# First shift and scale by feature tile with five sums at once, and the SSD Silu in three parts, in a fused four-layer network on one Trainium2 core

## The chip, the cores and the metric

The kernel runs on 1 core of one Trainium2 chip, as one launch. The metric is the device time in microseconds (us) from the start to the end of an execution; less is better. Engines are named as in the profile: PE is TensorE (matmul), PEld its weight loads, DVE VectorE, ACT ScalarE, POOL GpSimd, SP the queue that issues most DMAs.

## What is computed

Two small transformer-like blocks, one after the other, on 256 context and 256 latent tokens of width 1024. Every layer begins with adaLN: shift and scale come from `silu(c) @ ada_w + ada_b`, once for the context vector and once for the latent one. The change touches the first layer (gated linear attention, GLA) and the second (a state-space mixer, SSD):

```python
def modulate(h, shift, scale):
    return h * (1 + scale) + shift

# gla_mixer, for context and latent tokens
q, k, v, g, a = jnp.split(h @ w_in, split_at, axis=-1)      # 512, 512, 1024, 1024, 32 wide
logit = jnp.einsum('blzr,zrd->zbld', a.reshape(b, l, 2, GLA_RANK), w_a2) + b_a2[:, None, None, :]
log_a = jax.nn.log_sigmoid(logit.astype(jnp.float32)) / GLA_GATE_NORM
...                                                          # scans of 4 heads in both directions
# ssd_mixer
z, xbc, dt = jnp.split(h @ w_in, [SSD_DI, SSD_DI + SSD_CONV_DIM], axis=-1)
xbc = jax.nn.silu(dwconv(xbc, conv_w, conv_b))
xs, bm, cm = jnp.split(xbc, [SSD_DI, SSD_DI + SSD_GN], axis=-1)
...                                                          # chunked scan of 8 groups
return rms_norm(y * jax.nn.silu(z), norm_g) @ w_out, (s_f, s_b)
```

## The kernel before

All weights come from HBM in pieces of 128 rows by 1024 columns of f32 (512 KB). A large product is made from three: `load` fetches a piece into `wraw`, ACT writes its rounded part `whi` (line 419), DVE the remainder `wlo` (line 420), and `mm3` adds hi by hi, lo by hi and hi by lo into one PSUM bank (lines 441 to 443). Activations are kept the same way in pairs of big tiles. A Tile scheduler turns the written program into one in-order list for each engine; tile pools with a fixed number of buffers decide when a load may be issued.

**The start** (`layer0`, `half`, `gla`, `ada`). The generator `ada` streams each adaLN matrix in chunks: chunk c holds 1024 output features and comes in 8 pieces along the 1024 inputs, into 3 buffers `araw`. A piece costs four f32 products of a 32-column stationary tile `s` with 256 moving columns (line 541), each in its own 32 columns of the array, and in the profile each is two instructions. After the 8 pieces DVE adds the bias, transposes, and copies shifts and scales to `mf` (lines 568, 570, 574). For the first layer `_ada_tiles` orders the features so that chunk 0 holds shift and scale of feature tiles 0 to 3, and chunk 1 those of tiles 4 to 7. So `half(0)` can build the first half of the modulated input `u` after 8 pieces, and `half(1)` the rest after 16 (lines 2081, 2086). Three sums are made meanwhile by `products`: `a` and head 0's `q` and `k`, each over 8 feature tiles, 72 matrix products of 128x512. The remaining adaLN chunks are fed in steps of one piece by `fill`, which counts them in `nstep`.

**GLA.** Then come the decay logits of head 0 (`logits`, line 829), v and g of head 0 (192 products of 256 columns), and four scans. `weave(scan(h), gemm(h + 1), 0.7, 0.3)` sets 0.7 steps of the next head's projections (`gemm_ws` for q and k, 48 products of 512 columns; `gemm_xs` for v and g, 192 of 256) and 0.3 adaLN pieces behind each step of the scan, so that PE has other work while ACT, DVE and POOL make what the scan needs. What is left over is appended behind the scan.

**SSD.** The same holds for 8 groups with `weave(scan(g), gemm(g + 1), 1.1, 0.3)`. `gemm(g)` projects x and the B part (through a five-tap convolution, lines 1193 to 1198, into `FZ[g]`, columns 0 to 1535), C (1536 to 1791) and z (1792 to 2303, copied by ACT, line 1212). `scan(g)` begins with one Silu over all 2304 columns (line 1220). Then twelve PE transposes of x and B follow (line 1229) in four groups of three, each evicted by ACT (line 1230), and everything else of the scan hangs on these. The group before ends with a gating on POOL (line 1315) and a Square on ACT (line 1346, `ysq`).

## Time and profile before

| | |
|---|---|
| runs shown | 2644.35, 2653.82, 2659.15 us (median 2653.82) |
| profiled execution | 2649.63 us, span of its instructions 2647.8 us |
| mean granted PE clock | 0.981 |
| busy PE, PEld, DVE, ACT, POOL | 2509.8, 2052.2, 1939.2, 1273.6, 632.1 us |
| start, to the last of the 72 products | 0 to 62.5 us |
| logits, v and g of head 0 | 62.8 to 87.8 us |
| scan of head 0, to the first product of the next scan | 87.8 to 161.0 us |
| SSD scans | about 828 to 1160 us |

All times in the rows are from the start of the span. Busy time of PE counts an instruction up to a modelled end, and matmuls overlap, so the step from one start to the next is the better measure of what a product costs in a row. A number in brackets behind a row is the idle time of that engine just before, with what ended it.

### The profile page before, as it was taken

Reading aid. Unit: us, or ns where it says so; the run is one execution under the profiler, and the core shown is the slowest. Engines: PE = TensorE matmul, PEld = TensorE weight load, DVE = VectorE, ACT = ScalarE, POOL = GpSimd, SP = SyncE. Lnnn points to the kernel's source line nnn. Section 1 sums busy time; section 2 is a strip of 40 time slices with the busy share of each in tenths; the row PEclk is TensorE's granted clock in tenths of the full one; section 3 lists DMA queues with packets and bytes.
Section 4 is the critical chain, followed back from the end, with each engine's and each line's share of the span. In section 5 each row is a group of like instructions: output and inputs, shape, how many; then the busy total and the mean of one; then the engine's idle time right before and its main releaser. Section 6 shows DMA issues by size and latency. Waiting matters only on the chain. (4 is left out here: it accounts for less than half of the span.)

```text
span 2647.8 us, 38382 instructions
## 1 busy us (share of the span) xinstructions
PE 2509.8 (95%) x14350; PEld 2052.2 (78%) x14350; DVE 1939.2 (73%) x2999; ACT 1273.6 (48%) x2027; POOL 632.1 (24%) x517
## 2 busy tenths in 40 slices
PE   6999999999999999889999999999998998999998
PEld 3877668887778777769988778888887776888886
DVE  3566787799988777776566457756448777999987
ACT  2433444222246666745544344322235445877875
POOL 1122334032332233323224023112114331000000
PEclk8999999999999999989999999999999998999999
DMA  8344565666652222255553224656534126999995
GB/s 278 122 140 138 186 212 189 224 219 205 201 182 77 88 85 68 80 175 188 183 179 105 87 80 160 199 187 207 181 98 158 56 73 211 337 333 352 333 334 217
DMA packets 137507, 471.67 MB, mean 178 GB/s; under 512 B 16544, under 2 KB 21792, under 8 KB 137056
## 3 DMA queue, kind: packets, MB, share of 16 engines
q1 hardware_dynamic: 131264, 458.34, 51.9%
q10 hardware_dynamic: 6048, 10.80, 1.2%
q8 instruction: 115, 1.88, 0.3%
q14 instruction: 80, 0.66, 0.1%
HBM read 467.96 MB, written 1.11 MB: 177 GB/s over the span
## 5 line engine op out<-in xcount | busy, mean ns | idle before, releaser
L419 ACT ACTIVATE whi<-wraw 128x1024 fp32r<-128x1024 f32 x472 | 492.0, 1047 | 567.3 <-PE b L443 235.7
L420 DVE TENSOR_TENSOR wlo<-wraw,whi 128x1024 fp32r<-128x1024 f32 x472 | 588.6, 1256 | 221.1 <-ACT whi L419 216.7
L441 PE MATMUL b<-whi,big 128*128 128x512 f32 (+1 forms) x1696 | 599.6, 355 | 9.6 <-DVE xn L1405 4.4
L442 PE MATMUL b<-wlo,big 128*128 128x512 f32 (+1 forms) x1696 | 590.0, 348 | 6.0 <-DVE wlo L420 6.0
L443 PE MATMUL b<-whi,big 128*128 128x512 f32 (+1 forms) x1696 | 588.9, 347 | 0.6 <-POOL big L420 0.5
L441 PE MATMUL b<-big,whi 128*128 128x512 f32 (+1 forms) x1512 | 540.2, 359 | 8.7 <-ACT big L419 5.7
L443 PE MATMUL b<-big,wlo 128*128 128x512 f32 (+1 forms) x1512 | 531.0, 352 | 6.5 <-DVE wlo L420 6.5
L442 PE MATMUL b<-big,whi 128*128 128x512 f32 (+1 forms) x1512 | 532.4, 352 | 2.4 <-POOL big L420 2.2
L441 PEld LDWEIGHTS b<-whi,big 128*128 128x128 f32 x1696 | 323.6, 191 | 61.7 <-issue 14.4
L442 PEld LDWEIGHTS b<-wlo,big 128*128 128x128 f32 x1696 | 324.0, 191 | 46.7 <-DVE wlo L420 9.6
L443 PEld LDWEIGHTS b<-whi,big 128*128 128x128 f32 x1696 | 323.6, 191 | 40.3 <-issue 1.8
L441 PEld LDWEIGHTS b<-big,whi 128*128 128x128 f32 x1512 | 290.2, 192 | 56.2 <-issue 10.4
L443 PEld LDWEIGHTS b<-big,wlo 128*128 128x128 f32 x1512 | 290.8, 193 | 43.9 <-DVE wlo L420 8.2
L442 PEld LDWEIGHTS b<-big,whi 128*128 128x128 f32 x1512 | 291.1, 193 | 39.6 <-POOL big L420 5.0
L559 DVE SCALAR_TENSOR_TENSOR aacc<-wraw,s,aacc 128x1024 f32<-128x1024 f32 x161 | 233.0, 1474 | 40.3 <-DMA wraw<-in_ada 39.9
L420 DVE TENSOR_TENSOR wlo<-big,whi 128x1024 fp32r<-128x1024 f32 (+1 forms) x157 | 184.5, 1197 | 18.1 <-ACT whi L419 15.3
L420 POOL TENSOR_TENSOR big<-ut,big 128x256 fp32r<-128x256 f32 x101 | 106.3, 1061 | 381.4 <-ACT big L419 380.5
L419 ACT ACTIVATE whi<-big 128x1024 fp32r<-128x1024 f32 (+1 forms) x157 | 160.5, 1034 | 33.5 <-PE b L443 27.9
L420 POOL TENSOR_TENSOR big<-hr,big 128x512 fp32r<-128x512 f32 (+1 forms) x64 | 84.8, 1326 | 343.1 <-ACT big L419 314.4
L1198 DVE SCALAR_TENSOR_TENSOR FZ<-xp,vecs,FZ 128x512 f32<-128x512 f32 (+1 forms) x128 | 110.8, 866 | 11.3 <-ACT FZ L1196 10.1
L419 ACT ACTIVATE big<-ut 128x256 fp32r<-128x256 f32 x156 | 62.4, 413 | 85.8 <-DVE ut L676 28.1
L761 DVE TENSOR_TENSOR yt<-b,gate 128x512 f32<-128x512 f32 x92 | 63.0, 685 | 25.0 <-PE b L443 22.1
(449 smaller groups left out, 3524.4 us busy)
## 6 DMA issues: line engine op xcount, KB each, us to landing
big<-in_moe SPq DMA_DIRECT2D x148, 512.0 KB, 6.2
wraw<-in_f SPq DMA_DIRECT2D x136, 512.0 KB, 4.2
wraw<-in_ada SPq DMA_DIRECT2D x120, 512.0 KB, 4.3
araw<-in_ada SPq DMA_DIRECT2D x72, 512.0 KB, 4.4
wraw<-in_moe SPq DMA_DIRECT2D x72, 512.0 KB, 6.6
wraw<-in_g SPq DMA_DIRECT2D x68, 512.0 KB, 3.9
Hc<-in_moe SPq DMA_DIRECT2D x36, 512.0 KB, 6.4
wraw<-in_gla_o SPq DMA_DIRECT2D x16, 512.0 KB
```

The lines of the kernel that those rows point to most:

```text
L419: self.nc.scalar.activation(hi, t, AF.Copy)
L420: (eng or self.nc.gpsimd).tensor_tensor(lo, t, hi, op=OP.subtract)
L441: mm(ps, a[0], b[0], start=first, stop=False)
L442: mm(ps, a[0], b[1], start=False, stop=False)
L443: mm(ps, a[1], b[0], start=False, stop=last)
L559: nc.vector.scalar_tensor_tensor(acc[v], raw, s, acc[v], op0=OP.mult, op1=OP.add)
L761: nc.vector.tensor_mul(y, ps, gt)
L1198: V.scalar_tensor_tensor(o, xp[:, :ns, k:k + 256], w(k), o, op0=OP.mult, op1=OP.add)
```

## The change

`_ada_tiles` goes; all adaLN chunks are in plain order, and the first two, (0, 0) and (0, 1), are no longer made by `ada` (`nstep` starts at 16). A new array `head` holds the same 2048 features by feature tile: for tile k two pieces (half the inputs each) with the 128 shifts and 128 scales of that tile. `head_load` fetches them through seven buffers: the three `araw` and four that later serve the exponents (`eq`, `ek`). `head` makes 32 products of 64 moving columns for a tile (16 a piece), and DVE adds, transposes and copies 64 columns. `begin(k)` and `make` build feature tile k of `u` at once, both token halves by one ACT and one DVE instruction (before: two of each half as wide, every other tile's by POOL). Five sums are open at once: `a` and q and k of heads 0 and 1, so `products(k)` is 15 matrix products, 120 in all. Heads 0 and 1 then bring only v and g to the weave: 48 products of 512 columns leave the scan of head 0. In `ssd` the Silu of a group is three instructions: x and B, C, z.

```diff
+    def head_load(self, k, pool):
+        ts = []
+        for h in range(2):
+            n = (2 * k + h) % 7 - 3
+            ts.append(self.ar.tile([128, 1024], F32, name="araw") if n < 0 else
+                      pool.tile([128, 1024], F32, name="hraw", tag=("eq", "ek")[n % 2], bufs=2))
+            self.nc.sync.dma_start(ts[h], self.A["head"][k, h])
+        return ts
+
+    def head(self, k, ts, bias):
+        o = slice(64 * k, 64 * k + 64)
+        ps = self.adb.rearrange("p a b -> p (a b)")
+        for r in range(8):
+            for q in range(4):
+                t = ts[r // 4].rearrange("p (r q n) -> p r q n", r=4, q=4)
+                nc.tensor.matmul(ps[32 * q:32 * q + 32, o], self.s[0][:, r, :], t[:, r % 4, q, :], start=r == 0, stop=r == 7)
+        ev = self.tmp.tile([128, 256], F32, name="ut", bufs=3)[:, :64]
+        nc.vector.tensor_add(ev, ps[:, o], bias[:, o])
+        tr = self.tmp.tile([128, 256], F32, name="ut", bufs=3)[:, :64]
+        nc.vector.transpose(out=tr, in_=ev)
+        nc.vector.tensor_copy(self.mf[0][:, k:k + 9:8, :], tr.rearrange("p (a b) -> p a b", a=2)[:, :, 0:2])
...
-            if h:
+            if h > 1:
                 yield from self.gemm_ws(self.A["gla_qk"][h], u, ev)
...
-        first = gemm(0)
-        next(first)
-        b = [self.bank(self.pat), self.bank(self.pmm), self.bank(self.pmm)]
+        first = [gemm(h) for h in range(2)]
+        b = [self.bank(p) for p in (self.pat, self.pmm, self.pmm, self.pat, self.ptp)]
...
+        def products(k):
             for m, ps in enumerate(b):
+                h, j = (m - 1) // 2, (m - 1) % 2
+                self.mm3(ps, ws["a"](128 * k, 128) if m == 0 else ws[h, k // 4](256 * (k % 4) + 128 * j, 128),
+                         (u[0][:, k, :], u[1][:, k, :]), k == 0, k == 7)
+        make = {}
+        for k in range(3):
+            make[k] = begin(k)
+            weights(k)
+        for k in range(8):
+            make[k]()
+            if k:
+                products(k - 1)
+            if k < 5:
+                make[k + 3] = begin(k + 3)
+            if k in (1, 3):
+                weights(k // 2 + 3)
+        products(7)
...
-            self.weave(scan(h), gemm(h + 1), *PACE[0])
+            self.weave(scan(h), gemm(h + 1) if h else first[1], *PACE[0])
...
-            nc.scalar.activation(F, F, AF.Silu)
+            for o in (slice(0, 1536), slice(1536, 1792), slice(1792, 2304)):
+                nc.scalar.activation(F[:, o], F[:, o], AF.Silu)
...
+            def make():
+                self.head(k, ts, bias)
+                sc = self.sm.tile([128, 2], F32, name="sc0")
+                nc.vector.tensor_scalar(sc, self.mf[0][:, 8 + k, :], 1.0, None, op0=OP.add)
+                t = self.tmp.tile([128, 512], F32, name="xr", tag="y2k", bufs=3)
                 for p in range(2):
                     s = slice(256 * p, 256 * p + 256)
+                    nc.vector.tensor_scalar(t[:, s], xT[:, k, s], sc[:, p:p + 1], self.mf[0][:, k, p:p + 1], op0=OP.mult, op1=OP.add)
+                self.split(u[0][:, k, :], u[1][:, k, :], t, nc.vector)
```

In the lists below a name's number tells one buffer from another, and line numbers behind the change are higher by 2 in the helpers. The queue of SP at the start, before: the piece of `a`, the 8 pieces of chunk 0, the transposed input `xT`, head 0's first q and k weights, the 8 pieces of chunk 1.

```order
L431 DMA wraw<-in_gla_a 128x1024
L546 DMA araw<-in_ada 128x1024
L549 DMA abias<-in_adab 128x256
L546 DMA araw<-in_ada 128x1024 x7
L2079 DMA big_131<-in_xT 128x2048
L2089 DMA big_131<-in_xT 128x2048
L431 DMA wraw<-in_gla_qk 128x1024
L546 DMA araw<-in_ada 128x1024
L549 DMA abias<-in_adab 128x256
L546 DMA araw<-in_ada 128x1024 x7
L431 DMA wraw<-in_gla_qk 128x1024
```

The same place now:

```order
L592 DMA araw<-in_head 128x1024 x2
L2119 DMA big_131<-in_xT 128x1024
L433 DMA wraw<-in_gla_a 128x1024
L592 DMA araw<-in_head 128x1024
L592 DMA hraw<-in_head 128x1024
L433 DMA wraw<-in_gla_qk 128x1024
L592 DMA hraw<-in_head 128x1024 x2
L2119 DMA big_131<-in_xT 128x1024
L433 DMA wraw<-in_gla_qk 128x1024
L592 DMA hraw<-in_head 128x1024
L592 DMA araw<-in_head 128x1024 x3
L2119 DMA big_131<-in_xT 128x1024
```

The sequence now goes tile by tile, two pieces of `head` each, with `xT` in quarters and the five weight pieces in between.

PE near the end of the scan of head 0, before: the products of `out` (926), the logits of the next head (829), and projections of head 1 (441 to 443) between them.

```order
L926 MATMUL b<-big_134,AT 128x256
L926 MATMUL b<-S,QS 128x256
L829 MATMUL b<-wa_428,aT 64x128 x8
L441 MATMUL b<-whi,big_132 128x256
L442 MATMUL b<-wlo,big_132 128x256
L443 MATMUL b<-whi,big_133 128x256
L441 MATMUL b<-whi,big_132 128x256
L442 MATMUL b<-wlo,big_132 128x256
L443 MATMUL b<-whi,big_133 128x256
```

The same place now (951 is `out`, 854 the logits, 543 an adaLN piece, 909 the scores):

```order
L951 MATMUL b<-big_136,AT 128x256
L951 MATMUL b<-S,QS 128x256
L951 MATMUL b<-big_136,AT 128x256
L951 MATMUL b<-S,QS 128x256
L854 MATMUL b<-wa_700,aT 64x128 x8
L543 MATMUL ada<-araw,s_98 32x256 x4
L854 MATMUL b<-wa_700,aT 64x128 x8
L909 MATMUL b<-eq,ek 64x64 x10
L909 MATMUL b<-eq,big_136 64x64 x2
L909 MATMUL b<-big_136 64x64 x2
```

The projections of head 1 that stood here have moved ahead: the scan's own products and adaLN pieces follow each other directly.

ACT where an SSD group begins, before (1196 starts a convolution, 1278 writes the decay masks, 1212 evicts z):

```order
L1196 ACTIVATE FZ<-xp,vecs 128x256
L1278 ACTIVATE R<-tge,TH 128x128 x2
L1212 ACTIVATE FZ<-b 128x256
L419 ACTIVATE whi<-wraw 128x1024
L1346 ACTIVATE ysq<-big_6904 128x512
L419 ACTIVATE whi<-wraw 128x1024
L1212 ACTIVATE FZ<-b 128x256
L1220 ACT_TABLE_LOAD
L1220 ACTIVATE FZ<-FZ 128x2304
L1230 ACTIVATE big_6956<-b 128x384 x3
```

The same place now (1233, 1316, 1249, 1268 and 1384 are the former 1196, 1278, 1212, 1230 and 1346):

```order
L1233 ACTIVATE FZ<-xp,vecs 128x256
L1258 ACT_TABLE_LOAD
L1258 ACTIVATE FZ<-FZ 128x1536
L1249 ACTIVATE FZ<-b 128x256
L1316 ACTIVATE R<-tge,TH 128x128
L1258 ACTIVATE FZ<-FZ 128x256
L1316 ACTIVATE R<-tge,TH 128x128
L1384 ACTIVATE ysq<-big_7096 128x512
L421 ACTIVATE whi<-wraw 128x1024
L1249 ACTIVATE FZ<-b 128x256
L1268 ACTIVATE big_7148<-b 128x384
L1258 ACTIVATE FZ<-FZ 128x512
```

The table load and the Silu of x and B now stand ahead of both evictions of z and of the Square, the Silu of z behind the first eviction of transposes.

## Rows read from the trace of the kernel before

**Rows 1.** the page: busy time, share of the span, instructions of TensorE

```profile
PE 2509.8 (95%) x14350; PEld 2052.2 (78%) x14350; DVE 1939.2 (73%) x2999; ACT 1273.6 (48%) x2027; POOL 632.1 (24%) x517
```

**Rows 2.** waits of PE over the span: who for whom, total us, times, longest

```profile
PE ada L541 <- DMA araw<-in_ada: 17.7, 12, 8.0
PE b L1229 <- ACT FZ L1220: 11.8, 8, 1.9
```

**Rows 3.** stages of the start: busy us (instructions) of each engine, granted clock, DMA share, GB/s

```profile
0.00:10.00 10.00, 1.53 (x15) 0.43 (x16) 2.59 (x10) 2.66 (x4) 0.19 (x4) 1.00 0.74 254
...
20.00:30.00 10.00, 6.42 (x18) 3.38 (x19) 7.26 (x18) 3.82 (x9) 2.88 (x4) 1.00 1.00 382
...
50.00:60.00 10.00, 8.62 (x25) 6.27 (x25) 7.06 (x12) 4.50 (x9) 3.54 (x4) 0.60 0.78 260
```

**Rows 4.** timeline of the start (start, us taken): PE, from first piece to first product

```profile
8.03 1.08 PE L541 MATMUL ada<-araw,s 128*32 128x256 f32 x8 [8.03 <-DMA araw<-in_ada]
...
20.32 1.08 PE L541 MATMUL ada<-araw,s 128*32 128x256 f32 x8 [1.10 <-DMA araw<-in_ada]
...
24.26 0.79 PE L441 MATMUL b<-big,whi 128*128 128x512 f32 x1 [2.86 <-ACT big L419]
```

**Rows 5.** timeline of PE: products in a row, early and later, and the last adaLN piece

```profile
30.03 0.63 PE L442 MATMUL b<-big,whi 128*128 128x512 f32 x1
30.45 0.51 PE L443 MATMUL b<-big,wlo 128*128 128x512 f32 x1
...
33.18 0.39 PE L443 MATMUL b<-big,wlo 128*128 128x512 f32 x1
33.41 0.40 PE L441 MATMUL b<-big,whi 128*128 128x512 f32 x1
...
45.63 1.08 PE L541 MATMUL ada<-araw,s 128*32 128x256 f32 x8 [2.19 <-DMA araw<-in_ada]
```

**Rows 6.** timeline of PE: last product of the start, first of v, first of scan 0

```profile
62.46 0.39 PE L443 MATMUL b<-big,wlo 128*128 128x512 f32 x1
...
64.67 0.38 PE L441 MATMUL b<-whi,big 128*128 128x256 f32 x1
...
87.80 0.39 PE L857 MATMUL b<-gmq,ghi 128*128 128x512 f32 x1
```

**Rows 7.** timeline of PE in scan 0: 64-column products, the longest wait, the next scan

```profile
102.25 0.69 PE L884 MATMUL b<-eq,ek 128*64 128x64 f32 x16
...
153.30 0.65 PE L903 MATMUL b<-ident,ek 128*128 128x128 f32 x2 [0.97 <-DVE ek L900]
...
160.98 0.58 PE L857 MATMUL b<-gmq,ghi 128*128 128x512 f32 x1
```

**Rows 8.** stage: the last part of scan 0 (columns as in rows 3)

```profile
128.40:161.00 32.60, 31.63 (x289) 24.38 (x287) 21.90 (x50) 14.95 (x20) 7.02 (x6) 1.00 0.44 139
```

**Rows 9.** timeline at the start of SSD group 1: DVE, ACT, PE

```profile
862.78 1.01 DVE L1198 SCALAR_TENSOR_TENSOR FZ<-xp,vecs,FZ 128x256 f32<-128x256 f32 x2
...
866.49 0.63 ACT L1346 ACTIVATE ysq<-big 128x512 f32<-128x512 f32 x1 [2.00 <-POOL big L1315]
867.03 1.04 ACT L419 ACTIVATE whi<-wraw 128x1024 fp32r<-128x1024 f32 x1
867.98 0.36 ACT L1212 ACTIVATE FZ<-b 128x256 f32<-128x256 f32 x1
868.36 1.28 ACT L1220 ACT_TABLE_LOAD   x1
869.66 2.12 ACT L1220 ACTIVATE FZ<-FZ 128x2304 f32<-128x2304 f32 x1
872.42 0.87 ACT L1230 ACTIVATE big<-b 128x384 f32<-128x384 f32 x2 [0.64 <-PE b L1229]
...
864.80 0.40 PE L441 MATMUL b<-big,whi 128*128 128x512 f32 x1
...
871.83 0.88 PE L1229 MATMUL b<-ident,FZ 128*128 128x128 f32 x6 [1.86 <-ACT FZ L1220]
```

More of the change, by code (lines that the diff above doesn't have):

```diff
@@ L93, in _col @@
     return np.asarray(v).reshape(-1, 128).T
-def _ada_tiles(L, c):
-    return [8 * a + 4 * c + k for a in range(2) for k in range(4)] if L == 0 and c < 2 else list(range(8 * c, 8 * c + 8))
 def _gla_consts():
@@ L153, in layout @@
             for c in range(6):
-                ft = _ada_tiles(2 * b + i, c)
+                ft = list(range(8 * c, 8 * c + 8))
                 r[i, c] = w[i][:, :, ft].transpose(0, 1, 3, 2, 4)
@@ L158, in layout @@
         A[f"adab{b}"] = rb.reshape(2, 6, 128, 256)
+        if b == 0:
+            h = w[0][:, :, :16].reshape(2, 4, 128, 2, 8, 4, 32).transpose(4, 0, 2, 1, 5, 3, 6)
+            A["head"] = _f(h.reshape(8, 2, 128, 1024))
+            hb = np.zeros((4, 32, 8, 2, 32), v.dtype)
+            hb[:, :2] = v[0, :16].reshape(2, 8, 4, 32).transpose(2, 1, 0, 3)[:, None]
+            A["headb"] = hb.reshape(128, 512)
     w = g("gla_w_in")[0]
@@ L380, in setup @@
         self.steps = self.ada()
-        self.nstep, self.cap = 0, CAPS[0]
-        self.ada_done = set()
+        self.nstep, self.cap = 16, CAPS[0]
+        self.ada_done = {(0, 0), (0, 1)}
     def open_ada(self, bufs):
@@ L530, in ada @@
             b, i = divmod(L, 2)
-            for c in range(6):
+            for c in range(2 if L == 0 else 0, 6):
                 ps = self.adb[:, n % 2, :]
@@ L571, in ada @@
                 tr = tr.rearrange("p (a b) -> p a b", a=8)
-                ft = _ada_tiles(L, c)
-                for h in range(2):
-                    nc.vector.tensor_copy(self.mf[L][:, ft[4 * h]:ft[4 * h] + 4, :], tr[:, 4 * h:4 * h + 4, 0:2])
+                nc.vector.tensor_copy(self.mf[L][:, 8 * c:8 * c + 8, :], tr[:, :, 0:2])
                 self.ada_done.add((L, c))
@@ L780, in project, with gla @@
                 self.flush()
-    def gla(self, u, half, pool, sg, vq, i):
+    def gla(self, u, begin, pool, sg, vq, i):
         nc, V = self.nc, self.nc.vector
@@ L956, in scan, with weights @@
             yield from out(3, f3, sb)
-        first = gemm(0)
-        next(first)
-        b = [self.bank(self.pat), self.bank(self.pmm), self.bank(self.pmm)]
-        def products(kh):
-            w = ws[kh]
-            for m, ps in enumerate(b):
-                for kk in range(4):
-                    k = 4 * kh + kk
-                    self.mm3(ps, wl(128 * k, 128) if m == 0 else w(256 * kk + 128 * m - 128, 128),
-                             (u[0][:, k, :], u[1][:, k, :]), k == 0, k == 7)
-                    yield
-                if kh:
-                    ev_a(0, ps) if m == 0 else evs[0](m - 1, ps)
-        wl = self.load(self.A["gla_a"], 1024)
-        self.fill(8)
-        half(0)
-        ws = [self.load(self.A["gla_qk"][0][:, :1024], 1024)]
-        self.weave(products(0), iter(()), 0, 0.67)
-        self.fill(16 - self.nstep)
-        ws.append(self.load(self.A["gla_qk"][0][:, 1024:], 1024))
-        half(1)
-        drain(products(1))
+        first = [gemm(h) for h in range(2)]
+        for f in first:
+            next(f)
+        b = [self.bank(p) for p in (self.pat, self.pmm, self.pmm, self.pat, self.ptp)]
+        ws = {}
+        def weights(n):
+            if n == 0:
+                ws["a"] = self.load(self.A["gla_a"], 1024)
+            else:
+                h, kh = (n - 1) % 2, (n - 1) // 2
+                ws[h, kh] = self.load(self.A["gla_qk"][h][:, 1024 * kh:1024 * kh + 1024], 1024)
+        def products(k):
+            for m, ps in enumerate(b):
+                h, j = (m - 1) // 2, (m - 1) % 2
[14 more added lines that the diff above has]
+        products(7)
+        ev_a(0, b[0])
+        for m in range(4):
+            evs[m // 2](m % 2, b[m + 1])
         mq = pool.tile([128, 512], F32R, name="gmq")
@@ L2071, in layer0, with begin @@
         pool, pes = self.pool("gla")
[L2072 removed]
+        sg = self.big(1, 0)
+        xT = sg.rearrange("p (a b) -> p a b", a=8)
         u = self.new_u(0)
[L2075 to L2082 removed]
+        bias = pool.tile([128, 512], F32, name="hbias", tag="lsm")
+        nc.scalar.dma_start(bias, self.A["headb"])
+        def begin(k):
+            ts = self.head_load(k, pool)
+            if k % 2 == 0:
+                nc.sync.dma_start(sg[:, 512 * k:512 * k + 1024], self.A["xT"][:, 512 * k:512 * k + 1024])
+            def make():
[3 more added lines that the diff above has]
+                t = self.tmp.tile([128, 512], F32, name="xr", tag="y2k", bufs=3)
                 for p in range(2):
                     s = slice(256 * p, 256 * p + 256)
[L2085 to L2090 removed]
+                    nc.vector.tensor_scalar(t[:, s], xT[:, k, s], sc[:, p:p + 1], self.mf[0][:, k, p:p + 1], op0=OP.mult, op1=OP.add)
+                self.split(u[0][:, k, :], u[1][:, k, :], t, nc.vector)
+            return make
+        y, acc, w = self.gla(u, begin, pool, sg.rearrange("p (h t d) -> p h t d", h=4, t=4), self.big(1, 1), 0)
         pes.close()
```

18 lines of the change are left out of this document (2 added, 16 removed).

## Prediction

> **What bounds the kernel now.** I read the page first: PE counts as busy 95% of the span, DVE 73%, ACT 48% [rows 1]. So the product engine sets the time nearly everywhere, and only two things shorten it: fewer products, or fewer stretches in which PE stands. The waits of PE come next. The two longest groups are the two places of this change: 17.7 us on adaLN pieces from HBM, at the start, and 11.8 us on the Silu of eight SSD groups [rows 2]. The stages of the start then show that PE is not the bound there: 1.53 us busy in the first 10 us, with the DMA engines at 254 GB/s, while later in the start they reach 382 GB/s at full share [rows 3]. The timeline gives the shape: pieces arrive from 8.03 us on, the eighth is used at 20.32, the first product follows at 24.26 [rows 4]; the second chunk's last piece is used at 45.63 [rows 5], the last of 72 products starts at 62.46, and the first product of v at 64.67 [rows 6]. So two chains of "chunk, then DVE, then products" stand one behind the other. From 64.67 to 87.80 PE runs 192 products of v and g without a wait, 0.12 us each [rows 6].
>
> **The start, term by term.** What must arrive before the last tile of `u`: 16 pieces of `head`, 4 quarters of `xT` and 5 weight pieces, 25 x 0.524 MB = 13.1 MB, with about 0.6 MB of vectors. At 382 GB/s that is 35.9 us. The first 10 us moved 2.54 MB, worth 6.6 us at that rate, so the flow in effect begins at 3.4 us [rows 3], and the last piece lands at about 39.3 us. Before, three buffers held the flow back; now seven take turns, and a piece waits for the use of the one seven earlier. If only this counted, the end would be 39.3 plus a half piece (0.6), the chain from the last adaLN product (20.32 + 1.08) to the first product at 24.26, 2.86 us [rows 4], and 15 products of 0.23 us (33.18 to 33.41 [rows 5]), together 46.2 us.
>
> PE's own work is the other bound. 120 products x 0.23 = 27.6 us. A half piece is 32 instructions, four side by side. The trace of before has no 64-column product in 32-column groups; the nearest row is the scores, 16 instructions two by two in 0.69 us with their last latency [rows 7]. That is eight rounds of 64 columns, as a half piece has, so it costs 0.46 to 0.69 us; I take 0.57, and 16 of them are 9.1 us. These 36.7 us are at the upper of PE's two levels, 2.4 GHz. In the trace products took 0.42 us a step up to 30.45 us and 0.23 us later [rows 5], after PE had worked without a long pause since 24.26 [rows 4]. Here the first tile is ready at about 11.5 us, so I let the lower level hold to about 18 us: some 10 products and 5 half pieces at double price, 4.8 us. PE's order adds waits of about 3 us: for the first tile, and for the fifth weight piece, whose split waits until one of the four `whi` buffers is free. With the first half piece at 6.5 us: 6.5 + 36.7 + 4.8 + 3 = 51 us. PE's bound is the later one; I take 51, with v starting 2.2 us later as before (62.46 to 64.67), at 53.2. **Gain 11.5 us**; ends 6.5 us (lower level to 25 us) and 16.3 us (DMA alone).
>
> The rest of the start is off this path. DVE's additions, transposes and copies are a quarter as wide but eight times instead of twice, within the 4 us that a tile has. POOL's splits move to DVE. The gap before logits stays, since `a` is still finished first.
>
> **The scan of head 0.** 48 products of 512 columns have moved into the start: 48 x 0.23 = 11.0 us less PE work between 87.80 and 160.98 [rows 6, 7]. They also covered waits. The weave keeps its pace, so v and g of head 1 take the earlier places and the last part is left bare; the order shows outputs, logits, adaLN pieces and scores without projections between. Before, that part took 32.6 us, with DVE busy 21.9 of them [rows 8]. Less 11.0 us it would be 21.6 us. DVE loses about 4 us there, since evictions and weight splits come earlier, so some 18 of 21.6 us remain: tight. The longest wait before was 0.97 us, a transpose behind DVE [rows 7]. I count three more such waits, 3 us. **Gain 8 us**, ends 4 and 11.0.
>
> **The SSD groups.** Before, ACT copies the last of z at 867.98, loads the table (1.28 us) and runs the Silu (2.12 us) to 871.78; PE, in the projections of the next group since 864.80, waits 1.86 us for it [rows 9]. This recurs in seven groups; the first waits 0.2 us. x and B are ready earlier: DVE's taps at 862.78 are already the 256-wide ones of C [rows 9]. Now table and first Silu stand ahead of z and of the Square. 1536 columns cost at most 0.63 + 1.04 = 1.67 us by the 512- and 1024-wide rows [rows 9], so they end near 865.5. The first three transposes are due at 864.80, six products apart from the next. But their evictions stay behind the Square, which waits for POOL until 866.49, a weight split and the copy of z: about 868.4 [rows 9]. With few banks, the third and fourth group of transposes then wait, about 0.7 and 0.3 us, and the first 0.3 to 0.7. Net 1.86 plus some 0.4 of smaller waits less 1.3 is about 1.1 us a group. **Gain 8 us** for seven; ends 2 (evictions worse) and 13 (nothing new). The first group gains two table loads from the exponentials between its Silus, 2.6 us on ACT; its transposes come earlier, so I count zero.
>
> The cut itself costs ACT 1.67 + 0.36 + 0.63 against 2.12, at most 0.54 us a group, beside PE, with ACT idle half the time. The Trainium skill, "ScalarE: Activation LUTs" (What ACT_TABLE_LOAD costs), speaks against cutting: each ACTIVATE has a fixed 186 ns besides 0.833 ns an element. By it the three parts take an estimated 2.48 us, and eight groups would lose 2.9 us if ACT set the time, a gain of 24.6 us instead of 27.5. The row agrees on the whole (186 + 1920 = 2106 ns against 2.12 us [rows 9]); PE waiting only for the first part decides for the sum.
>
> **The sum.** 11.5 + 8 + 8 = 27.5 us off the span of 2647.8: 2620.3, and 1.8 us around it, 2622.1 us. The median of the runs lies 4.2 us above the profiled execution, which would make it 2626.3. I name 2624.
>
> **The rivals.** *One part fails.* Evictions give back the SSD gain, or bare waits take the scan's: 27.5 less 6 to 14, 2632 to 2640 us. For it: DVE near full in rows 8, the Square in rows 9. Against: the waits are on other engines than the one relieved. *The clock stays low in the start.* Then 120 x 0.42 + 16 x 1.14 + 9.5 = 78 us, v at about 80: 15 us lost, 16 gained elsewhere, 2649 us, no change. For it: after a pause for pieces PE was back at 1.08 us for a piece at 45.63 [rows 5], and 50 to 60 us shows a granted clock of 0.60 [rows 3]. Against: a tile brings PE 4.6 us of work at the upper level for 4.4 us of DMA (1.64 MB), so from the second tile on it hardly pauses. *Slower: the low level lasts through v and g.* Its 192 products at 0.24 instead of 0.12 us add 23 us more: 2672 us. It decides from about 14 us of this, six tenths of those products; before, PE came up in the midst of the second half's products, so I hold it unlikely. The Trainium skill, "TensorE: Matmul & The Clock Gate" (HAM oscillation), has a rule for this pair: a product loop that waits for DMA between tiles can fall to half clock at every tile. By that rule these two cases would be the likely ones; the trace shows the fall after waits, but not with PE loaded this densely. *The change does not do what it says*: the order shows both moves, so no chance of its own.
>
> **Chances.** Forecast 0.70 (2611 to 2633), one part fails 0.18, low clock in the start 0.07, slower 0.04, more than all upper ends 0.01. A measurement of this kernel tells about 0.5%, 13 us, from no change. Faster 0.87, within 0.09, slower 0.04. The range runs from all upper ends, 2609, to one part failing, 2639.
>
> **What would show it.** Start: first product of v near 53 us (48 to 58), DMA near 380 GB/s to 40 us, steps of 0.23 us from about 18 us. Scan of head 0: some 65 us instead of 73.2. SSD: the 11.8 us of waits on the Silu below 4, new ones on the evictions of transposes. Wrong would be 0.42 us steps beyond 30 us, a scan of 73 us, or groups as long as before.

## The result

The changed kernel takes 2611.92 us (median of four runs, 2609.45 to 2616.57), against 2650.45 us before (four runs): a ratio of 0.9863, 95% interval 0.9845 to 0.9881. The prediction was 2624 us, range 2609 to 2639. The time lies in the range, near its lower end, and the direction was right. Two of the three terms were not: the start gave half of what I had put down, the SSD groups twice as much.

The page of the profile after, the span and the engines (it answers to [rows 1]):

```profile
span 2608.7 us, 39146 instructions
PE 2493.8 (96%) x14734; PEld 2049.2 (79%) x14734; DVE 1939.6 (74%) x2999; ACT 1276.7 (49%) x2038; POOL 622.6 (24%) x509
```

The waits of PE after (who for whom, total us, times, longest; they answer to [rows 2]):

```profile
PE ada L603 <- DMA araw<-in_head: 6.5, 2, 6.2
...
PE b L443 <- ACT whi L421: 5.4, 1, 5.4
...
PE b L1267 <- ACT big L1268: 1.9, 1, 1.9
```

The wait on the Silu is gone from the list; of 11.8 us nothing is left but one wait of 1.9 us on the eviction of the last group's transposes. The waits on adaLN pieces fell from 17.7 to 6.5 us, and 6.2 of these are the time to the first piece. But a new one stands beside them: 5.4 us, once, for `whi`.

To see where the 39.1 us of the span went, I matched the products of both traces one by one and took the difference of their start times. This table is worked out so; each row is the part that a stretch adds.

| stretch (times of before) | gained, us |
|---|---|
| start, to the first product of v at 64.67 | 5.5 |
| v and g; scan of head 0; edge to the next scan, to 170 | 12.3 |
| to the end of that layer and to SSD, 828 | 1.4 |
| SSD and the projection behind it, to 1165 | 18.0 |
| one wait near 1637 | 2.5 |
| all the rest | -0.5 |

Each row is one pair of executions. With the second trace of each kernel (below) the start gains 4.7 us and not 5.5, the SSD stage some 20.4 and not 18.0. The start before is the less steady of the two: in four traces its first product of v comes at 61.7 to 64.7 us, in four traces with the new start, otherwise unaltered, at 58.8 to 59.2.

The stages of the start (busy us and instructions of PE, PEld, DVE, ACT, POOL, granted clock, DMA share, GB/s; they answer to [rows 3]):

```profile
0.00:10.00 10.00, 2.16 (x64) 1.71 (x64) 1.36 (x9) 1.60 (x3) 0.19 (x4) 1.00 0.80 284
10.00:20.00 10.00, 5.97 (x75) 3.69 (x79) 5.26 (x15) 2.84 (x4) 0.00 (x0) 1.00 1.02 411
20.00:30.00 10.00, 9.21 (x103) 6.31 (x102) 4.96 (x10) 2.00 (x3) 0.00 (x0) 1.00 1.02 405
30.00:40.00 10.00, 10.00 (x212) 7.75 (x211) 5.95 (x17) 2.21 (x3) 0.00 (x0) 1.00 0.81 293
```

The DMA engines run at their full share from 10 to 30 us, and from 20 us on PE is busy. The bound is PE, as forecast. The timeline of the start (start, us taken; in brackets the idle time before and what ended it; it answers to [rows 4 to 6]):

```profile
6.15 1.08 PE L603 MATMUL ada<-araw,s 128*32 128x64 f32 x32 [6.15 <-DMA araw<-in_head]
7.56 1.08 PE L603 MATMUL ada<-araw,s 128*32 128x64 f32 x32 [0.33 <-DMA araw<-in_head]
10.69 0.23 DVE L605 TENSOR_TENSOR ut<-ada,hbias 128x64 f32<-128x64 f32 x1 [7.36 <-DMA hbias<-in_headb]
...
14.03 0.80 PE L443 MATMUL b<-big,whi 128*128 128x512 f32 x1 [5.39 <-ACT whi L421]
...
18.95 0.63 PE L443 MATMUL b<-big,whi 128*128 128x512 f32 x1
19.38 0.63 PE L444 MATMUL b<-big,whi 128*128 128x512 f32 x1
...
20.94 0.73 PE L445 MATMUL b<-big,wlo 128*128 128x512 f32 x2 [0.36 <-DVE wlo L422]
21.61 0.52 PE L603 MATMUL ada<-hraw,s 128*32 128x64 f32 x18
...
34.74 0.50 PE L443 MATMUL b<-big,whi 128*128 128x512 f32 x1
35.08 0.40 PE L444 MATMUL b<-big,whi 128*128 128x512 f32 x1
35.31 0.39 PE L445 MATMUL b<-big,wlo 128*128 128x512 f32 x1
...
59.16 0.38 PE L443 MATMUL b<-whi,big 128*128 128x256 f32 x1
```

Three things are to be seen. The first tile's adaLN products are through at 8.64, but DVE adds the bias at 10.69: it waited for the load of `hbias`, 256 KB, which was issued at 2.13. I had not priced that load at all. The steps of products are 0.43 us at 19 us and 0.23 at 35: the lower level of PE's clock (1.2 GHz), which lasted to about 20 us. The two products from 20.94 to 21.61 already take 0.67 us together, less than two steps of 0.43. And a step straight behind a half piece takes 0.34 us (34.74 to 35.08), the next one 0.23.

One SSD group after (it answers to [rows 9]; line 1386 is the Square, which in all groups but the first writes `Hc`, and line 1353 is POOL's gating ahead of it):

```profile
880.00 1.49 ACT L1258 ACTIVATE FZ<-FZ 128x1536 f32<-128x1536 f32 x1 [0.46 <-DVE FZ L1235]
...
883.22 0.42 ACT L1258 ACTIVATE FZ<-FZ 128x256 f32<-128x256 f32 x1 [1.18 <-DVE FZ L1235]
...
883.53 0.73 POOL L1353 TENSOR_TENSOR big<-big,FZ 128x256 f32<-128x256 f32 x1 [5.91 <-DVE xp L1229]
883.55 0.49 PE L1267 MATMUL b<-ident,FZ 128*128 128x128 f32 x3
...
884.29 0.63 ACT L1386 ACTIVATE Hc<-big 128x512 f32<-128x512 f32 x1 [0.36 <-POOL big L1353]
...
886.04 0.48 ACT L1268 ACTIVATE big<-b 128x384 f32<-128x384 f32 x1
886.41 0.63 ACT L1258 ACTIVATE FZ<-FZ 128x512 f32<-128x512 f32 x1
...
886.99 0.49 PE L1267 MATMUL b<-ident,FZ 128*128 128x128 f32 x3
```

The Silu of x and B ends at 881.49, 2 us before PE comes to the transposes. The first eviction ends at 886.52, half a microsecond before PE's third group of transposes. PE stands nowhere in these rows. From the first transposes of one group to those of the next are now 37.5 us (the first interval 36.7, the last 37.8); before, three of the seven intervals were 40.0 to 40.1 us and four 41.1 to 41.4.

### The profile page after: what moved, and what is told of

It is laid out like the page before. It is cut to its first block, busy times and chain, and to the rows that moved or that the text cites. A ratio compares the mean times of both kernels' runs of the same rounds, so it can differ in the third digit from the quotient of the medians.

```text
span 2608.7 us, 39146 instructions
## 1 busy us (share of the span) xinstructions
PE 2493.8 (96%) x14734; PEld 2049.2 (79%) x14734; DVE 1939.6 (74%) x2999; ACT 1276.7 (49%) x2038; POOL 622.6 (24%) x509
## 4 chain that ended last, share of the span: by engine, by line
PE 53%; DVE 8%; issue 3%; ACT 3%; POOL 2%; DMA 1%; DVEq 0%; POOLq 0%; ACTq 0%; SPq 0%
PE b L443 15%; PE b L444 15%; PE b L445 15%; DVE FZ L1235 2%; DVE wlo L422 2%; PE b L1465 1%; POOL hrs L1440 1%; ACT whi L421 1%; PE b L1496 1%; PE b L1484 1%; PE b L1999 1%; PE b L2076 1%; PE b L1278 0%; PE b L1344 0%; PE b L1347 0%
## 5 line engine op out<-in xcount | busy, mean ns | idle before, releaser
L561 DVE SCALAR_TENSOR_TENSOR aacc<-wraw,s,aacc 128x1024 f32<-128x1024 f32 x161 | 229.8, 1454 | 39.6 <-DMA wraw<-in_ada 39.1
L422 POOL TENSOR_TENSOR big<-ut,big 128x256 fp32r<-128x256 f32 x93 | 98.6, 1068 | 335.0 <-ACT big L421 334.0
L1235 DVE SCALAR_TENSOR_TENSOR FZ<-xp,vecs,FZ 128x512 f32<-128x512 f32 (+1 forms) x128 | 109.1, 853 | 20.6 <-ACT FZ L1233 19.5
L421 ACT ACTIVATE big<-ut 128x256 fp32r<-128x256 f32 x140 | 56.5, 412 | 62.1 <-DVE ut L701 25.6
```

The lines of the kernel that those rows point to most:

```text
L421: self.nc.scalar.activation(hi, t, AF.Copy)
L422: (eng or self.nc.gpsimd).tensor_tensor(lo, t, hi, op=OP.subtract)
L561: nc.vector.scalar_tensor_tensor(acc[v], raw, s, acc[v], op0=OP.mult, op1=OP.add)
L1235: V.scalar_tensor_tensor(o, xp[:, :ns, k:k + 256], w(k), o, op0=OP.mult, op1=OP.add)
```

## The experiments

Fourteen traces are compared: those of the two kernels and of twelve runs, of which one is the kernel before and one the changed kernel again. Where a ratio to the kernel before is given below, it comes from four executions; the second run of the kernel before and the kernels with more products, with the Silu in two parts, with three buffers, with the bias first and with 20 idle products were executed once, and only their traces are read. The times in this table are read from the traces: the first product of v, the length of the scan of head 0, the interval from one SSD group's transposes to the next's (the value most of the seven intervals have), and the span.

| kernel | first v | scan 0 | SSD group | span |
|---|---|---|---|---|
| before | 64.67 | 73.18 | 40.0 and 41.1 | 2647.8 |
| before, again | 63.57 | 73.19 | 40.0 and 41.1 | 2650.6 |
| changed | 59.16 | 62.58 | 37.5 | 2608.7 |
| changed, again | 58.86 | 62.82 | 37.5 | 2611.2 |
| Silu cut alone | 63.60 | 73.19 | 37.5 | 2627.5 |
| new start alone | 58.80 | 62.87 | 40.0 (last 41.6) | 2627.2 |
| three sums | 51.58 | 73.18 | 37.5 | 2620.4 |
| eight products more in each scan | 61.72 | 73.18 | 41.6 and 43.1 | 2655.8 |
| Silu in two parts | 58.79 | 63.97 | 37.5 (last 39.3) | 2609.0 |
| three buffers | 60.39 | 63.86 | 37.5 | 2613.6 |
| bias first | 57.32 | 63.04 | 37.5 | 2608.7 |
| 20 idle products | 58.79 | 62.54 | 37.5 | 2614.9 |
| bias first, 18 idle products | 57.69 | 62.98 | 37.5 | 2612.2 |
| bias first, 28 idle products | 56.25 | 63.86 | 37.5 | 2613.4 |

The two pairs of equal kernels tell what a span is worth: 2.5 to 2.8 us lie between two profiled executions of the same program, and the four runs of the changed kernel differ by up to 7.1 us. Part of this lies in the very stages of the change: the second execution of the kernel before reaches v 1.1 us earlier, and the second of the changed kernel takes 2.4 us less in the SSD stage.

### The two parts, each alone

The kernel before with the cut Silu:

```diff
-            nc.scalar.activation(F, F, AF.Silu)
+            for o in (slice(0, 1536), slice(1536, 1792), slice(1792, 2304)):
+                nc.scalar.activation(F[:, o], F[:, o], AF.Silu)
```

> The kernel before with the SSD Silu in three parts and nothing else. Theory A (the stage's gain is the wait on the Silu and the low clock that follows the wait in four of the groups): a group takes 37.5 us instead of 40.0 to 41.1, the granted clock stays at 1.00 in the stage, PE's waits on the Silu fall from 11.8 us to below 2, and the total falls by 18 us, a ratio of 0.993. Theory B (my prediction's size: 8 us for the cut; what the stage gained beyond that came with the shift of everything ahead of it): groups near 39 us, 8 us in all, 0.997.

Measured: 0.9934 (0.9917 to 0.9950), 37.5 us in each group but the first (36.6), the granted clock at 1.00 through these intervals. Theory A: the stage gives some 17 us with the old start too.

The changed kernel with the Silu whole (the same edit backwards):

> The changed kernel with the SSD Silu undivided again. Theory A (the two parts add up): first product of v at 59.2 us, scan of head 0 in 62.6 us, SSD groups at 40.0 to 41.1 us with waits of 1.86 us on the Silu; 20 us less than before, a ratio of 0.9925. Theory B (the SSD stage gains from the new start too): 28 us less, 0.9895.

Measured: 0.9945 (0.9929 to 0.9962), first product of v at 58.80 us, scan of head 0 in 62.87, PE waits on the Silu of 11.8 us in eight groups. The parts add up within their intervals: 0.0066 and 0.0055 against 0.0137 for both. The ratio of 0.9925 that Theory A named lies outside, so by its runs the new start alone is worth some 15 us and not 20 (its trace gives 20.6). And one thing was not expected. Six of the seven intervals are 40.0 us and only the last 41.6, though the same waits stand in both kernels: 0.2 us in the first group, 1.85 in the next six, 0.5 in the last. Stages of the kernel before in its second execution, then one of this kernel (columns as above):

```profile
914.00:954.00 40.00, 37.29 (x214) 30.87 (x213) 30.96 (x56) 27.22 (x53) 13.12 (x11) 1.00 0.24 80
994.00:998.00 4.00, 3.52 (x15) 3.18 (x16) 1.76 (x3) 2.56 (x6) 0.00 (x0) 0.61 0.24 83
1035.00:1076.00 41.00, 38.39 (x212) 32.32 (x212) 31.12 (x56) 27.49 (x53) 12.95 (x11) 0.96 0.23 78
```

```profile
892.00:932.00 40.00, 37.28 (x212) 30.85 (x212) 30.96 (x56) 27.22 (x53) 13.14 (x11) 1.00 0.23 80
```

In the kernel before, PE's clock fell behind the wait in four groups: the granted clock is 0.61 over 4 us, with steps at the lower level (1.2 GHz). Those are the four intervals above 41 us. Here one is left. Against this kernel the cut is worth 15 us (it lies 0.2 us ahead of the changed kernel before the stage and 14.8 us behind it after); the other 3 of the 18 us fit the three falls of 1.1 us that only the kernel before had.

### Is the fall of the clock chance, and can the wait be filled?

The kernel before, once more, unchanged:

> The kernel before, unchanged, profiled once more. In its first profile four of the seven whole SSD groups took 41.1 us instead of 40.0, with a granted clock of 0.96 or less behind the wait for the Silu; with the new start and the old Silu none of six did, though the same waits of 1.86 us were there. Theory A (a wait of this length can be followed by a fall, and which one is differs from execution to execution): again some groups of 40.0 and some of 41.1 us, not the same ones. Theory B (the fall belongs to what is running in groups three to seven of the kernel before): the same four groups at 41.1 us.

Theory B: the same four groups, within 0.05 us (41.10, 41.08, 41.06, 41.35). So at this place it was the same in both executions, and yet three of these waits do without it where they come 19 us earlier. Elsewhere two executions of one program do differ. In the scan of head 0 the changed kernel has a wait of 1.29 us on DVE (131.32 in its first trace): there the granted clock stays at 1.00, but in its second execution it is 0.72 from 130 to 136 us. Of the nine traces with this scan seven show the fall, and their scan takes 62.8 to 64.0 us; the two without it take 62.5 and 62.6. What decides on a fall I cannot say from these runs.

The kernel before with eight products more in each scan:

```diff
             nc.scalar.activation(F, F, AF.Silu)
+            pt = self.bank(self.ptp)
+            for _ in range(8):
+                mm(pt, u[0][:, 0, 0:128], u[0][:, 0, :], start=True, stop=True)
```

> The kernel before with eight more products of 512 columns (1.84 us), which nothing reads, in every SSD scan ahead of the transposes, so that PE works in the time in which it waited 1.86 us for the Silu. Theory A (PE's clock falls because PE stands those 1.86 us, and the fall costs 1.1 us a group in four groups): the granted clock stays at 1.00 and all groups take 40.0 us, some 4 us less than before though 64 products are added. Theory B (the clock's fall there has nothing to do with the wait): groups of 40.0 and 41.1 us as before, the same total; if the products lie beside no wait, 14.7 us more.

Neither came as it stands. One group of it:

```profile
904.17 1.06 ACT L419 ACTIVATE whi<-wraw 128x1024 fp32r<-128x1024 f32 x1 [2.50 <-PE b L442]
...
905.53 2.00 PE L1223 MATMUL b<-big 128*128 128x512 f32 x8
...
907.22 0.63 ACT L1351 ACTIVATE Hc<-big 128x512 f32<-128x512 f32 x1 [1.99 <-POOL big L1318]
907.37 0.39 PE L441 MATMUL b<-big,whi 128*128 128x512 f32 x1
...
910.32 0.39 PE L442 MATMUL b<-big,whi 128*128 128x512 f32 x1
910.39 2.12 ACT L1220 ACTIVATE FZ<-FZ 128x2304 f32<-128x2304 f32 x1
912.56 0.87 PE L1232 MATMUL b<-ident,FZ 128*128 128x128 f32 x6 [1.86 <-ACT FZ L1220]
```

The eight products ran, and the wait behind them was 1.86 us as before; a group took 41.6 us, 1.6 more. But they did not fill the wait. From 905.53 to the wait PE has 22 products of 512 columns here, the eight and 14 of the next group; before, from 864.80 [rows 9], it has 22 of the next group. In PE's order the eight took the places of eight others, and these moved behind the transposes. So the group became longer by work behind the transposes, and what products in the wait itself would cost stays open. What the rows show is the chain ahead of the Silu in ACT's order: a weight split that waits for PE's products (904.17), a Square that waits for POOL (907.22), another split, a copy of z. It is as long as before, 6.2 us from the first split to the Silu. That the falls of the clock come from PE's standing stays unproven too: this kernel kept its waits, and two of its seven intervals were 43.1 us.

### Where to cut

```diff
-            for o in (slice(0, 1536), slice(1536, 1792), slice(1792, 2304)):
+            for o in (slice(0, 1536), slice(1536, 2304)):
```

> The changed kernel with the SSD Silu in two parts, x and B in the first, C and z together in the second. Theory A (the only cut that matters is the one behind x and B): SSD groups of 37.5 us as with three parts, the total within 2 us. Theory B (C has to come before z, since the products of C with B stand behind the transposes): a wait on the second part, groups of 38 us or more.

Theory A: six of the seven intervals are as with three parts, and the trace lags the changed kernel by 1.1 us ahead of the stage and behind it (from the scan of head 0). The last interval is 39.3 us, with a fall of the clock in it, but that is made up by the end of the stage. In this one execution the third part does nothing.

### Five sums or three

The changed kernel with `a`, q and k of head 0 only; q and k of head 1 go back into the weave:

```diff
-            if h > 1:
+            if h:
                 yield from self.gemm_ws(self.A["gla_qk"][h], u, ev)
...
-        b = [self.bank(p) for p in (self.pat, self.pmm, self.pmm, self.pat, self.ptp)]
+        b = [self.bank(p) for p in (self.pat, self.pmm, self.pmm)]
...
-            self.weave(scan(h), gemm(h + 1) if h else first[1], *PACE[0])
+            self.weave(scan(h), gemm(h + 1), *PACE[0])
```

> The changed kernel with three sums at once in the start instead of five: q and k of head 1 are projected beside the scan of head 0 again, as before the change; the features still come tile by tile. Theory A (the two more sums only move 48 products, 11 us, from the scan to the start, and the gain is that of the tiles): first product of v at about 48 us, scan of head 0 at about 73 us, the total within 3 us of the changed kernel. Theory B (the two sums fill time in which PE would stand waiting for tiles): first product of v at about 53 us, scan of head 0 at 73, 5 to 8 us more than the changed kernel.

Measured: 0.9894 (0.9877 to 0.9910), so 8 us above the changed kernel by the ratios, whose intervals overlap at their ends; the traces lie 9 to 12 us apart. First product of v at 51.58 us, scan of head 0 in 73.18. That is Theory B in the total, at the upper end of its 5 to 8 us. In v, 51.58 isn't quite comparable: here the first products of v stand ahead of the logits, which end at 54.64, and in the changed kernel behind them. The waits of PE in its first 80 us, and the stages from the last sums on:

```profile
PE b L443 <- ACT big L421: 4.2, 5, 1.5
PE b L445 <- DVE wlo L422: 1.2, 1, 1.2
```

```profile
52.00:56.00 4.00, 4.00 (x42) 3.53 (x42) 3.66 (x5) 2.94 (x5) 0.00 (x0) 0.94 0.38 121
56.00:60.00 4.00, 4.00 (x24) 4.00 (x24) 2.08 (x4) 3.95 (x5) 0.00 (x0) 0.63 0.88 254
```

With three sums a tile brings PE too little work. PE waits for the next tile (4.2 us on `u`, against 0.6 in the changed kernel), stands 1.3 us just before the end, and the granted clock falls to 0.63 in v. From the first product of v to the scan are 27.4 us, against 23.1; some 2.5 of the 4.3 us more are the logits that lie within, and some 1.5 the fall, 16 products at 0.21 us instead of 0.12. That is a short piece of the rival "the low level lasts through v and g" of the prediction. None of the nine traces with five sums has a fall between its last sums and the scan. The Trainium skill, "TensorE: Matmul & The Clock Gate" (HAM oscillation), tells of a loop whose work for a tile is shorter than the DMA wait for the next, and which starts every tile at the lower clock. The trace differs: a tile's work, about 3.2 us (9 x 0.23 + 2 x 0.56), was longer than each wait (1.5 us at most), the clock fell once, and what PE waited for was ACT's and DVE's work on `u`, not a DMA.

### What held the start back

Three buffers instead of seven for the pieces of `head`:

```diff
-            n = (2 * k + h) % 7 - 3
-            ts.append(self.ar.tile([128, 1024], F32, name="araw") if n < 0 else
-                      pool.tile([128, 1024], F32, name="hraw", tag=("eq", "ek")[n % 2], bufs=2))
+            ts.append(self.ar.tile([128, 1024], F32, name="araw"))
```

> The changed kernel with the pieces of head in the three buffers araw alone, not in seven. Theory A (the four more buffers are what brings the pieces in time; with three a piece can be fetched only when the one three earlier is used): the DMA engines fall below 350 GB/s between 10 and 30 us, PE waits for pieces, the first product of v at 63 us or later instead of 59.2. Theory B (PE's order is behind the pieces from the first tile on, so that three buffers do): v within 1 us of 59.2.

```profile
10.00:20.00 10.00, 6.09 (x85) 3.90 (x85) 5.58 (x15) 3.17 (x4) 0.00 (x0) 1.00 0.70 268
20.00:30.00 10.00, 8.96 (x92) 6.00 (x93) 4.62 (x10) 1.67 (x3) 0.00 (x0) 1.00 0.94 333
```

Between the two: the flow is slower as A said (268 and 333 GB/s, against 411 and 405), but v starts at 60.39, only 1.2 us later. PE's waits for pieces are 7.4 us against 6.5. So PE's order was the bound for the most part, not the arrival of pieces.

The first tile's bias first on ACT's queue:

```diff
+        nc.scalar.dma_start(self.hbias[:, :64], self.A["headb"][:, :64])
         nv = sum(w for _, w in self.vat.values())
...
-        nc.scalar.dma_start(bias, self.A["headb"])
+        nc.scalar.dma_start(bias[:, 64:], self.A["headb"][:, 64:])
```

> The changed kernel with the load of the bias of the first feature tile (64 columns, 32 KB) put first on ACT's queue; the other 448 columns stay where all 512 stood. Theory A (the first tile is late because DVE's addition waits until 10.69 us for the bias, 2 us after the tile's last adaLN product): the addition at 8.7 us, the first matrix product at 12 instead of 14.03 us, the first product of v at 57 instead of 59.2 us. Theory B (behind the bias the weights of the sum a or the transposed input are late as well): the first matrix product not before 13.5 us, v at 58.7 us or later.

```profile
8.36 0.22 DVE L608 TENSOR_TENSOR ut<-ada,hbias 128x64 f32<-128x64 f32 x1 [2.37 <-PE ada L606]
...
9.85 0.73 DVE L2131 TENSOR_SCALAR xr<-big,sc,mf 128x256 f32<-128x256 f32 x2 [0.59 <-DMA big<-in_xT]
...
12.25 0.79 PE L446 MATMUL b<-big,whi 128*128 128x512 f32 x1 [3.96 <-ACT whi L424]
```

Theory A: first matrix product at 12.25 us, first product of v 1.8 us earlier than in the changed kernel. The next late thing is the transposed input, 0.59 us.

Idle products of a zero tile while PE stands, ten before the first piece and ten before the first matrix product:

```diff
+        V.memset(u[1][:, 7, :].bitcast(F32), 0.0)
+        def warm(n):
+            for _ in range(n):
+                mm(b[4], u[1][:, 7, 0:128], u[1][:, 7, :], start=True, stop=True)
+        warm(10)
         for k in range(8):
             make[k]()
+            if k == 0:
+                warm(10)
```

> The changed kernel with 20 products of 512 columns of a zero tile, which nothing reads, on PE where it stands: ten before the first adaLN piece and ten before the first matrix product (at 0.43 us each 4.3 us in 6.1, and 4.3 us in 5.4). Theory A (products take 0.43 us up to 22 us because PE stands most of the first 14 us, and that costs some 4 us): steps of 0.23 us from 15 us at the latest, the first product of v at 55 us instead of 59.2. Theory B (the low level of the start lasts to 22 us whatever PE does before): steps of 0.43 us to 22 us as in the changed kernel, v at 59 to 60 us.

```profile
2.65 4.12 PE L1010 MATMUL b<-big 128*128 128x512 f32 x10 [2.65 <-DVE big L1006]
6.70 1.30 PE L603 MATMUL ada<-araw,s 128*32 128x64 f32 x64
7.94 2.56 PE L1010 MATMUL b<-big 128*128 128x512 f32 x10
13.61 0.79 PE L443 MATMUL b<-big,whi 128*128 128x512 f32 x1 [3.11 <-ACT whi L421]
```

Neither as it stands. The first ten brought PE up: the second ten took 2.56 us, 0.23 a product. But being faster they left a pause of 3.11 us, and products went at 0.43 us again, with a granted clock of 0.50 between 14 and 18 us. So the next two kernels have the bias first as well, and fill the pause with 8 and with 18:

> The changed kernel with both: the first tile's bias first on ACT's queue, and 18 idle products (ten before the first adaLN piece, eight before the first matrix product). Theory A (both costs are real and lie one behind the other): the first product of v at 53 us, which is where my prediction had put it, and 6 us less in all than the changed kernel. Theory B (with an earlier PE the adaLN pieces from HBM end last): v at 55 us or later, 3 us less at most.

Measured for this first of the two: 0.9872 (0.9853 to 0.9891); v at 57.69 us. That is Theory B's number, but not its reason: eight left a pause of 1.97 us, and the clock fell again.

> As the kernel with the first tile's bias first and the idle products, but 18 instead of 8 of them between the first tile's adaLN products and the first matrix product. With 8, PE came up to steps of 0.23 us at 8.3 us, stood for 1.97 us before the first matrix product at 12.38 and went at 0.43 us a step again from 14 to 21 us. Theory A (that pause is what PE falls on, and the low level then costs some 3 us): no pause, steps of 0.23 us from 8 us on, the first product of v at 54 to 55 us instead of 57.7, and some 4 us less in all than the changed kernel. Theory B (the waits of 0.4 to 0.7 us for weights between 14 and 16 us are enough for the fall, or the tiles then come too late): steps of 0.43 us again before 20 us, v at 57 to 58 us.

```profile
8.61 4.37 PE L1013 MATMUL b<-big 128*128 128x512 f32 x18
...
13.50 0.50 PE L446 MATMUL b<-big,whi 128*128 128x512 f32 x1
...
15.71 0.50 PE L446 MATMUL b<-big,whi 128*128 128x512 f32 x1 [0.66 <-ACT whi L424]
...
17.99 0.73 PE L448 MATMUL b<-big,wlo 128*128 128x512 f32 x2 [0.73 <-DVE wlo L425]
```

Theory A in its mechanism: steps of 0.23 us from 8 us on, through waits of 0.7 us. In size between the two: v at 56.25 us, 2.9 us before the changed kernel. A faster PE now waits for the weights' splits at 15.7 and 18. 1.3 us of this were lost again in the scan of head 0 (63.86 us against 62.58), where the clock fell at the wait on DVE. In all the runs gave 0.9863 (0.9843 to 0.9884), no different from the changed kernel:

> The changed kernel once more, beside the others: the first product of v at 59.2 us, some 2612 us. It shows what a difference of a few us to it is worth, and whether the clock in the SSD stage reads 1.00 again.

Measured: 0.9866 (0.9848 to 0.9884); v at 58.86, the SSD groups at 37.5 us with a granted clock of 1.00. The 2.9 us are as large as the difference between two executions of one program, so none of these versions can be said to beat the changed kernel. They are there to size the terms.

## Why the prediction came out, step by step

**The start: too much, by 6 us.** Forecast were v at 53.2 us and a gain of 11.5, ends 6.5 and 16.3; measured 59.16 and 5.5, below the lower end, as with every pair of traces above. The working was 6.5 + 36.7 + 4.8 + 3. The first half piece came at 6.15. The work itself was right: steps of 0.23 us, and the last 352 products of the pieces took 6.18 us, 0.56 a half piece. So was the lower level: the nine products and three half pieces between 14.03 and 22.06 would take 3.8 us at the upper level and took 7.7 without the one wait of 0.36, and the first two half pieces took 1.0 us more than later ones; 4.9 us together. The step that failed is "waits of about 3 us". They were 6.7: 5.39 for the first tile, ready at 14 and not 11.5, and 1.3 of smaller ones. Two us of it are the bias, a load that the diff shows and that I had counted among "0.6 MB of vectors" without asking when it lands. What is left, 6.15 + 36.7 + 4.9 + 6.7 against 56.94, where the last product of the sums ends, is 2.5 us, and no term of mine had it. 1.7 us of it are sixteen changes between the narrow and the wide products, at each of which one step is 0.1 us longer (34.74 to 35.08 above); 0.5 more are longer steps beside waits.

The rival "clock stays low in the start" did not come; PE came up at about 20 us. Its neighbour, a low level in v and g, showed only with three sums.

**The scan of head 0: right, a little low.** Forecast a gain of 8 us, 65 us long; measured 10.6, at 62.6 us, and 12.3 with the edge to the next scan. The 48 products are worth 11.2 us by their own steps in both traces (512-column products of later heads in the scan and its edge: 72 in 17.7 us before, 24 in 6.5 after). Within the scan alone there are only 43 fewer, since products of head 2 moved up into it. New waits came, as counted, the longest on DVE where the rival had placed it:

```profile
131.32 0.80 PE L909 MATMUL b<-eq,ek 128*64 128x64 f32 x20 [1.29 <-DVE big L957]
```

In scan and edge the waits of PE are 4.0 us, against 2.5 before, with the 0.97 us of [rows 7] among those that went. So they cost 1.4 us and not 3. The 112 products of adaLN pieces there gave something back, 8.0 us by their steps against 10.3, the waits left out; why, I have not tested. Together 11.2 - 1.4 + 2.3 make the 12.3 with 0.2 of small differences.

**The SSD groups: too little, by 10 us.** Forecast 8 us, ends 2 and 13; measured 18. Per group I had 1.86 plus 0.4 less 1.3 of new waits. My own sum was off: that is 0.96 and not "about 1.1", 6.7 us for seven groups. And the wait of 1.86 us stands in six groups and not in seven; the last has 0.5. The first two terms were right: 2.02 us with the restart and 0.46 of slower transposes make the 2.48 between 40.0 and 37.5. The step that failed is the 1.3: I let the evictions stay behind a Square that waits for POOL, 3.6 us behind the transposes' due time, and they come 2.5 us behind it (886.04). The third group of transposes, 3.44 us behind the first, then finds its bank free. The gating on POOL starts where I had it, at the first transposes' due time (864.80 before, 883.55 now), but it takes 0.73 us and not 1.68:

```profile
864.78 1.68 POOL L1315 TENSOR_TENSOR big<-big,FZ 128x256 f32<-128x256 f32 x1 [5.91 <-DVE xp L1192]
```

That is 0.95 of the 1.1 us, and it holds in each of the later groups, with the cut Silu alone too. I had taken the price of POOL's instruction from the old trace, where DVE runs a weight split beside it (864.64 to 865.86); in the new one DVE's next split starts only at 885.90. Whether that is the reason I have not tested. Six intervals at 2.48 are 14.9 us and the last group brought some 2; 2.6 us were given back just behind the stage, where PE now stands 1.05 us for DVE, which waits for a gate vector from HBM, and 0.94 us for a weight split. That is about the 15 us of the cut. The falls of the clock, 1.1 us each, I had not seen at all: I read one group, one without a fall [rows 9], and took it for all.

The rival "one part fails" did not come: the evictions gave nothing back. What the cut costs ACT is as forecast: 1.49 + 0.42 + 0.63 = 2.54 us against 2.12, beside PE. The Trainium skill, "ScalarE: Activation LUTs" (What ACT_TABLE_LOAD costs), gave an estimated 2.48 by its fixed part for each instruction, and the trace agrees; the loss of 2.9 us that I had worked out from it did not show, since PE waits only for the first part.

**Outside the change, 2.5 us.** Near 1637 us the kernel before has a wait of 1.85 us on DVE's RMS normalization and a granted clock of 0.66 behind it; the changed kernel has two shorter waits there and no fall. The edit doesn't touch that place. The new start with the old Silu has the loss too, the cut Silu alone has not, but neither has the kernel with eight more products and the old Silu. Why stays open.

**The sum** came into the range partly by luck, because the errors had two signs: 27.5 - 6 (start) + 10 (SSD) + 4.3 (scan and its edge) + 1.4 (rest of the layer) + 2.5 - 0.5 (outside) = 39.2 us. I had the places and the bound of each right, and the sizes of two wrong. Without the error in the start the time would have been about 2606 us, below the range.

## What to carry to other kernels

When one engine waits for a large instruction of another and needs only a part of its result, cut the instruction there and put that part first in the order; here this took the wait out of every group. When products are added to fill a wait, read from the new order what they displaced: here eight others moved behind the wait's end, the wait stayed, and the group became longer. For a start that is fed tile by tile, open enough sums that each tile's products outlast the making of the next tile, and list for the first tile every load that it needs with its own landing time, small vectors too: a small one issued beside large ones can land with them. And read a term from several groups and, where there are any, several executions before pricing it.

## What the hardware did that was not expected

- A load of 256 KB issued at 2.13 us, with some 1.8 MB issued before it on both queues, was there only at 10.69 us. Its first 32 KB, put ahead, cost DVE no wait at 8.36.
- Behind equal waits of 1.85 us PE's clock fell in four SSD groups of the kernel before, the same four in two executions, and in only the last of them where the waits came 19 us earlier. Each fall cost 1.1 us behind it, over half of the wait itself. At a wait of 1.29 us in the scan of head 0 it fell in one execution of the changed kernel and not in the other.
- The same POOL instruction on 128x256 took 1.68 us in the SSD groups before and 0.73 us after, where no weight split of DVE ran beside it.
- In the start idle products brought PE to 0.23 us a product at 8 us instead of about 20. It kept that through waits of 0.4 to 0.7 us, and lost it after pauses of 1.97 and 3.11 us. The granted clock in the rows of the changed kernel reads 1.00 there all the same, with steps of 0.43 us for 512 columns (1.2 GHz); only the rows of the kernels with idle products show 0.50.
